# Attention rounds of a hybrid decoder block: the products with V between the two halves of the transposes, the copies of the second half behind the round's end

## The chip, the cores and the metric

The kernel runs on one core of one Trainium2 chip. The metric is the time of one execution in microseconds (us) on the device. Work is spread over five engines that run side by side, each through its own list of instructions in order: TensorE (PE, matmuls and transposes; PEld is its weight load), VectorE (DVE), ScalarE (ACT), GpSimd (POOL) and SyncE (SP, here only the issuer of transfers). They wait for each other through semaphores.

## The reference, cut to what matters

One decoder block on a sequence of 2048 positions and 1024 channels, in float32. One input projection gives the inputs of two branches. Branch A is a causal sliding-window attention in three head groups with dilation 1, 4 and 16, eight heads of 64 channels each; branch B is a convolution with a gated linear recurrence. Both are gated, projected, merged, projected once more and normalised. The change lies in branch A, in this part of the reference:

```python
    s = jnp.einsum('brnqhd,brnkhd->brnhqk', qb, kw) * (Dh ** -0.5)
    ...
    s = jnp.where(valid[None, None, :, None], s, NEG_INF)
    m = jnp.max(s, axis=-1, keepdims=True)
    p = jnp.exp(s - m)
    l = jnp.sum(p, axis=-1, keepdims=True)
    o = jnp.einsum('brnqhk,brnkhd->brnqhd', p, vw)
```

Queries come in blocks of 128 (after the positions are regrouped by the dilation), and each block sees the keys of its own block and of the one before it, 256 in all. Where a block has no block before it (the first of each subsequence, and every block of the group with dilation 16) it sees 128 keys only.

## The kernel before, in words

The kernel has three stages. First the input projection (matmuls in a fast scheme with seven products, L622, with the convolution and the recurrence beside them), then the attention, then the projections of both branches, the merge and the normalisation (from L1305 on). Nothing in the order of instructions is left to a scheduler: every engine runs its instructions in the order in which the program writes them. What can shift is only what they wait for: data, and buffers that come round again.

The attention works through 12 units, one for each dilation group and pair of heads; `unit(u)` takes the groups in the order 1, 16, 4 in turn. Each unit has 2048 queries, cut in four rounds of 512, so there are `NG = 48` rounds; a round has four query blocks j = 0 to 3 and two heads h. The work on one round's data is spread over four rounds of the loop. The names of the steps:

- `scores(i)` (PE, L1005): 24 matmuls into four PSUM tiles "s" (two blocks and one head each). The pool has four such buffers, so the next round's scores wait until the peaks of this round have read them.
- `peak(i, j, h)` (DVE, L1012): adds the mask to one block's scores (kept with reversed sign), writes them to SBUF as "p" and accumulates their minimum. Its operand is 256 or 128 wide, as the block has one before it or not.
- `expo(i, j, h)` (ACT, L1020): the exponential in place on "p", and its sum.
- `turn(i, w)` (PE, L1030): transposes half w of a round (blocks 2w and 2w+1) into two PSUM tiles "pt", k = 0 and 1.
- `bring(i, w, k, eng)` (L1043 on ACT, L1045 on DVE): copies one such tile to SBUF, into "ptb". Of the first half, k = 0 goes to ACT and k = 1 to DVE; of the second half, k = 1 goes to DVE, and k = 0 goes to DVE in the "light" rounds (all of dilation 16, and every third of the others) and to ACT in the others.
- `values(i)` (PE, L1058): the products of "ptb" with V into one PSUM tile "o".
- `leave(i)` (DVE, L1067, L1069, L1071): copies "o" out to SBUF, from where it is sent to memory.

The tiles "pt" and "o" share one pool of PSUM buffers, tag "t", with four buffers that are given out in the order of the program; a round takes five (two, two and one). So a tile takes the buffer of the fourth one before it and waits until that one has been read out.

```python
        t = st["t", i, w] = [aps.tile([P, 2, 2, 2, 64], F32, tag="t", name=f"pt{i}{w}{k}", bufs=4) for k in range(2)]
        o = st["o", i] = aps.tile([P, 4, P], F32, tag="t", name=f"o{i}", bufs=4)
```

In round i of the loop PE has, in this order, the scores of i, the transposes of both halves of i-1, and the products of i-2. ACT has the last three exponentials of i-1, the first of i, the copy of the first half, three exponentials, the copy of the second half (unless the round is light), and one exponential. DVE has the copy-out of i-3, four peaks of i, its copy of the first half, two peaks, in a light round the other copy of the second half, two peaks, and its copy of the second half.

Of the kernel before, what the change touches and what calls it, by code (L numbers as in the profile page):

```python
# [31 lines left out]
def hybrid_block_kernel(ctx: ExitStack, tc: tile.TileContext, a: dict, out: bass.AP):  # L32
    nc = tc.nc
    sp, act, dve, pool, pe = nc.sync, nc.scalar, nc.vector, nc.gpsimd, nc.tensor
# [59 lines left out]
    def later(lag, fn):  # L94
        late.append((now["n"] + lag, fn))
# [4 lines left out]
    def run(queue):  # L100
        due = [x for x in queue if x[0] <= now["n"]]
        queue[:] = [x for x in queue if x[0] > now["n"]]
        for _, fn in due:
            fn()
# [443 lines left out]
    light = [("v", FT_V + 2 * j, FT_V + 2 * j + 1) for j in range(6)]  # L548
# [129 lines left out]
    def at(t, fn):  # L678
        events.setdefault(t, []).append(fn)
# [26 lines left out]
    for s, pl in enumerate(plan):  # L706
        if pl[4] == "ug" and not (pl[0] and pl[1][1][0] - FT_U in put_off):
            at(base[s] + 1, lambda i=pl[1][1][0] - FT_U: fetch_gr(i))
        if pl[0] and pl[4] == "ug":
            i = pl[1][1][0] - FT_U  # L710
# [4 lines left out]
    def keep_raw(b, c, kk):  # L715
        load_raw(b, c, kk, "c")

    def one_block(b, kk):
        if kk == 0:
            new_block(b)  # L720
        hi_lo(b, kk, xr["c" + b, kk])
        spend(ACT=.66, DVE=.72)
# [26 lines left out]
    def bring(t, b, c):  # L749

        at(t - 3, lambda: [keep_raw(b, c, kk) for kk in K4])
        at(t, lambda: [one_block(b, kk) for kk in K4])
# [36 lines left out]
    def unit(u):  # L789

        return (0, 2, 1)[u % 3], u // 3
# [41 lines left out]
    def v_parts(g, j):  # L833
        src = v_scr[g][j]

        def part(i):
            def fn():
                if i == 0:
                    VT[g, j] = big(VSLOT[g, j], [P, 16, 256], F32, f"V{g}{j}")
                V = VT[g, j]  # L840
                if g == 0:
                    sp.dma_start(V[:, 4 * i:4 * i + 4], src[i * CH:(i + 1) * CH].rearrange("(n p) f -> p n f", p=P))
                elif g == 1:
                    sp.dma_start(V[:, 4 * i:4 * i + 4], src[i * CH:(i + 1) * CH].rearrange("(j r) f -> j r f", r=4))
                else:
                    sp.dma_start(V[:, 4 * i:4 * i + 4], src.rearrange("(i r) f -> i r f", r=16)[:, 4 * i:4 * i + 4])
            return fn

        return [part(i) for i in range(4)]
# [115 lines left out]
    def prev(g, n):  # L965
        if g == 0:
            return n - 1 if n >= 1 else None
        if g == 1:
            return n - 4 if n >= 4 else None
        return None  # L970

    st = {}
# [3 lines left out]
    def first(i, j):  # L976
        u, q = divmod(i, 4)
        g, _ = unit(u)
        return 0 if prev(g, 4 * q + j) is not None else P
# [27 lines left out]
    def peak(i, j, h):  # L1007
        u, q = divmod(i, 4)
        lo = first(i, j)
        if h == 0:  # L1010
            st["p", i, j] = p_p.tile([P, 2, 256], F32, tag="p", name=f"p{i}{j}")
        dve.tensor_tensor_reduce(out=st["p", i, j][:, h, lo:256], in0=st["s", i, j // 2][h][:, j % 2, lo:256],  # L1012
                                 in1=mask[:, lo:256], scale=1.0, scalar=3e38, op0=ALU.add, op1=ALU.min,
                                 accum_out=sta[u][:, 4 * q + j, h:h + 1])

    def expo(i, j, h):
        u, q = divmod(i, 4)
        p = st["p", i, j][:, h, first(i, j):256]
        s = sta[u][:, 4 * q + j]
        act.activation(p, p, AF.Exp, scale=-1.0, bias=s[:, h:h + 1], accum_out=s[:, 2 + h:3 + h])  # L1020
# [9 lines left out]
                        pe.transpose(t[k][:, j % 2, x, h, :], pp[j % 2][r, h, x * P:(x + 1) * P], ident[r, r])  # L1030

    def bring(i, w, k, eng):
        if k == 0:
            st["b", i, w] = at_p.tile([P, 2, 2, 2, P], F32, tag="pt", name=f"ptb{i}{w}", bufs=4)
        src = st["t", i, w][k]
        dst = st["b", i, w][..., HALF[k]]
        lo = [first(i, 2 * w + j) // P for j in range(2)]
        if lo[1]:
            dst, src = (t[:, :, 1] for t in (dst, src))
        else:  # L1040
            dst, src = (t.rearrange("p j x h q -> p (j x) h q")[:, lo[0]:] for t in (dst, src))
        if eng is act:
            act.activation(dst, src, AF.Copy)  # L1043
        else:
            dve.tensor_copy(dst, src)  # L1045

    def values(i):
        u, q = divmod(i, 4)
        g, hp = unit(u)
        V = VT[g, hp // 2]  # L1050
        o = st["o", i] = aps.tile([P, 4, P], F32, tag="t", name=f"o{i}", bufs=4)
        for j in range(4):
            ptb = st["b", i, j // 2]
            n = 4 * q + j
            for x in range(first(i, j) // P, 2):
                for h, hs in enumerate(HALF):
                    v0 = P * (hp % 2) + 64 * h
                    pe.matmul(o[hs, j, :], V[:, n if x else prev(g, n), v0:v0 + 64], ptb[:, j % 2, x, h, :],  # L1058
                              start=(x == first(i, j) // P), stop=(x == 1))

    def leave(i):
        u, q = divmod(i, 4)
        g, hp = unit(u)
        o, t = st.pop(("o", i)), ot[u]
        cs = slice(q * CH, (q + 1) * CH)
        if g == 0:
            dve.tensor_copy(t[:, cs].rearrange("p (b q) -> p b q", b=4), o)  # L1067
        elif g == 1:
            dve.tensor_copy(t[:, cs].rearrange("p (j r) -> p j r", r=4), o.rearrange("p r j -> p j r"))  # L1069
        else:  # L1070
            dve.tensor_copy(t.rearrange("p (j r) -> p j r", r=16)[:, :, 4 * q:4 * q + 4], o.rearrange("p r j -> p j r"))  # L1071
        if g < 2:
            later(1, lambda: sp.dma_start(o_scr[g][hp][:, cs], t[:, cs]))
        elif q == 3:
            later(1, lambda: sp.dma_start(o_scr[g][hp], t))
        if q == 3:
            f0 = 4 * (3 * hp + g)
            dst = st_scr[:, f0:f0 + 4]
            if g == 0:
                later(1, lambda: sp.dma_start(dst.rearrange("(n q) f -> q n f", q=P), sta[u]))  # L1080
            elif g == 2:
                later(1, lambda: sp.dma_start(dst.rearrange("(q n) f -> q n f", q=P), sta[u]))
            else:
                for c in range(4):
                    later(1, lambda c=c: sp.dma_start(dst[c * CH:(c + 1) * CH].rearrange("(q r) f -> q r f", r=4),
                                                      sta[u][:, 4 * c:4 * c + 4]))
# [21 lines left out]
    def load_h(c, k, lag):  # L1108
        if k % 4 == 0:
            HH["t"] = big((("X3", "X4"), ("Z0", "Z1"))[c % 2][k // 4], [P, 4, 2, CH], F32R, f"h{c}{k}")  # L1110
        t = HH[c, k] = HH["t"][:, k % 4]
        sp.dma_start(flat(t[:, 1]), hb_scr[k * P:(k + 1) * P, c * CH:(c + 1) * CH])
        later(lag, lambda: split(t[:, 0], t[:, 1], dve if c else pool))

    NG = 48
# [4 lines left out]
    for i in range(NG + 3):  # L1120
        u = i // 4
        on, turns = i < NG, 0 < i <= NG
        run(late)
        if i in VORD:
            loads += v_parts(*VORD[i])
        if i % 4 == 0 and 1 <= u <= 9:
            loads += unit_parts(u + 2)
        for _ in range(2):
            if loads:
                loads.pop(0)()  # L1130
        if on:
            scores(i)
        if i > 2:
            leave(i - 3)
        if turns:
            expo(i - 1, 2, 1)
            expo(i - 1, 3, 0)
            expo(i - 1, 3, 1)
        if on:
            peak(i, 0, 0)  # L1140
            expo(i, 0, 0)
            for j, h in ((0, 1), (1, 0), (1, 1)):
                peak(i, j, h)
        if turns:
            turn(i - 1, 0)
            bring(i - 1, 0, 0, act)
            bring(i - 1, 0, 1, dve)
        if on:
            for j, h in ((0, 1), (1, 0), (1, 1)):
                expo(i, j, h)  # L1150
            peak(i, 2, 0)
            peak(i, 2, 1)
        if turns:
            turn(i - 1, 1)
            light = unit((i - 1) // 4)[0] == 2 or i % 3 == 0
            bring(i - 1, 1, 0, dve if light else act)
        if on:
            peak(i, 3, 0)
            peak(i, 3, 1)
            expo(i, 2, 0)  # L1160
        if turns:
            bring(i - 1, 1, 1, dve)
        if i > 1 and i - 2 < NG:
            values(i - 2)
        if i in (40, 41):
            prep_wl(i - 40, 2)
        if 42 <= i < 46:
            load_h(0, 2 * (i - 42), 2)
            load_h(0, 2 * (i - 42) + 1, 2)
        if i in (46, 47):  # L1170
            prep_wl(i - 44, 2)
        now["n"] += 1
# [308 lines left out]
    for tt in range(16):  # L1481
        c, b = divmod(tt, 4)
# [68 lines left out]
```

## Time and profile before

| | us |
|---|---|
| runs: median (lowest to highest of 3) | 2123.54 (2120.29 to 2123.6) |
| profiled execution, its own time | 2117.73 |
| its span from first to last instruction | 2116.0 |
| PE busy | 2083.6 (98%) |
| DVE busy | 1667.7 (79%) |
| ACT busy | 1123.4 (53%) |
| POOL busy | 490.1 (23%) |

The attention lies between about 1446 and 1659 us of the span: its first scores begin at 1445.7, and the first product of the stage behind it begins at 1658.60. Busy shares over the whole span say little about it, since the three stages have different limits; what is read below is the attention alone. In the answers of the trace a line gives start, duration, engine, line of the program, operation and the tiles written and read; what stands in brackets behind it is the idle time of the engine before it and what ended that. The durations of neighbouring instructions on one engine can overlap: an exponential is shown with 505 ns, while the next one starts 492 ns after it.

### The profile page before, as it was taken

How to read it: one execution, taken by the hardware profiler on the slowest of the kernel's cores; microseconds unless marked ns; L12 is line 12 of the kernel's file. 1: busy time of each engine (PE TensorE's matmuls, PEld its weight loads, DVE VectorE, ACT ScalarE, POOL GpSimd, SP SyncE). 2: the span in 40 equal slices, each digit the busy share in tenths (PEclk: the TensorE clock that was granted, in tenths of full speed). 3: DMA queues.
4: the chain of work that ended last, by engine and by line, in shares of the span. 5: the costliest groups of instructions: out<-in, count | busy, mean ns of one | idle time of the engine just before them, and what ended most of it. 6: DMA issues, size and time to landing. Idle time of an engine off the chain costs nothing.

```text
span 2116.0 us, 35899 instructions
## 1 busy us (share of the span) xinstructions
PE 2083.6 (98%) x12016; PEld 1723.9 (81%) x12016; DVE 1667.7 (79%) x3193; ACT 1123.4 (53%) x2348; POOL 490.1 (23%) x465
## 2 busy tenths in 40 slices
PE   8999999999999999999999999999999999999998
PEld 7888888888878888887888888888888888888887
DVE  8987888898888867787787887777999645576667
ACT  6356455357356565656567766667999411121100
POOL 1111111111111012231231232223535444332120
PEclk9999999999999999999999999999999999999999
DMA  8987997997997977677788788879988788874432
GB/s 271 280 259 225 281 277 212 285 288 230 276 289 230 331 219 202 214 238 211 249 255 269 255 254 265 259 224 383 293 305 260 227 278 282 293 250 158 164 110 70
DMA packets 345832, 524.69 MB, mean 248 GB/s; under 512 B 124208, under 2 KB 153904, under 8 KB 341808
## 3 DMA queue, kind: packets, MB, share of 16 engines
q1 hardware_dynamic: 325760, 489.54, 71.3%
q0 software_dynamic: 12256, 19.42, 5.6%
q10 hardware_dynamic: 7632, 13.44, 1.7%
q8 instruction: 96, 1.57, 0.3%
q14 instruction: 88, 0.72, 0.1%
HBM read 317.14 MB, written 190.45 MB: 240 GB/s over the span
## 4 chain that ended last, share of the span: by engine, by line
PE 64%; ACT 5%; DVE 3%; DMA 1%; issue 1%; SPq 0%; DVEq 0%; ACTq 0%
PE q L622 39%; ACT p L1020 3%; PE yb L1305 3%; PE yb L1306 3%; PE z L1415 3%; PE z L1416 3%; PE yb L1307 3%; PE z L1417 3%; PE ya L1383 1%; PE ya L1384 1%; PE ya L1385 1%; PE o L1058 1%; DVE p L1012 1%; ACT ptb L1043 1%; PE g L492 1%; PE s L1005 1%
## 5 line engine op out<-in xcount | busy, mean ns | idle before, releaser
L622 PE MATMUL q<-xT,hS 128*128 128x512 f32 x1680 | 521.1, 391 | 0.0
L622 PE MATMUL q<-xT,l 128*128 128x512 f32 x1120 | 436.0, 389 | 0.0
L622 PE MATMUL q<-xB,hA 128*128 128x512 f32 x1248 | 389.5, 393 | 5.7 <-ACT xB L215 5.7
L622 PEld LDWEIGHTS q<-xT,hS 128*128 128x128 f32 x1680 | 312.8, 188 | 69.0 <-issue 5.5
L622 PE MATMUL q<-xB,l 128*128 128x512 f32 x904 | 353.0, 391 | 0.0
L622 PEld LDWEIGHTS q<-xB,hA 128*128 128x128 f32 x1248 | 234.0, 189 | 57.2 <-ACT xB L215 5.7
L622 PEld LDWEIGHTS q<-xT,l 128*128 128x128 f32 x1120 | 210.2, 188 | 44.2
L622 PEld LDWEIGHTS q<-xB,l 128*128 128x128 f32 x904 | 170.4, 188 | 36.0
L245 POOL DMA_DIRECT2D wS<-in_w_in_dram x70 | 62.0, 969 | 493.7 <-DMA wS<-in_w_in_dram 139.0
L1020 ACT ACTIVATE p<-p,sta 128x256 f32<-128x256 f32 (+1 forms) x384 | 172.2, 456 | 4.8 <-DVE sta L1012 4.1
L622 PE MATMUL q<-xB,hS 128*128 128x512 f32 x560 | 174.1, 392 | 0.0
L622 PE MATMUL q<-xT,hA 128*128 128x512 f32 x560 | 173.0, 390 | 0.0
L269 ACT ACTIVATE hA<-wA 128x512 fp32r<-128x512 f32 x218 | 134.9, 623 | 53.2 <-DMA wA<-in_w_in_dram 23.8
L269 ACT ACTIVATE hS<-S 128x512 fp32r<-128x512 f32 x175 | 109.0, 623 | 79.4 <-DVE S L227 51.1
L227 POOL TENSOR_TENSOR S<-S,wA 128x512 f32<-128x512 f32 x35 | 45.5, 1299 | 392.8 <-DVE S L227 218.0
L622 PEld LDWEIGHTS q<-xT,hA 128*128 128x128 f32 x560 | 104.7, 188 | 23.0 <-issue 1.5
L622 PEld LDWEIGHTS q<-xB,hS 128*128 128x128 f32 x560 | 104.0, 188 | 22.4 <-issue 1.5
L1012 DVE CUSTOM_DVE_ANT_0 p<-s,mask 128x256 f32<-128x256 f32 (+1 forms) x384 | 118.7, 360 | 4.3 <-PE s L1005 3.3
L1416 PE MATMUL z<-wo,mh 128*128 128x512 f32 (+1 forms) x264 | 101.0, 383 | 0.0
L1417 PE MATMUL z<-wo,ml 128*128 128x512 f32 (+1 forms) x264 | 101.0, 383 | 0.0
L1415 PE MATMUL z<-wo,mh 128*128 128x512 f32 (+1 forms) x264 | 101.0, 383 | 0.0
L1305 PE MATMUL yb<-h,wl 128*128 128x512 f32 x256 | 100.3, 392 | 0.0
(201 smaller groups left out, 4208.5 us busy)
## 6 DMA issues: line engine op xcount, KB each, us to landing
wA<-in_w_in_dram SPq DMA_DIRECT2D x253, 256.0 KB, 4.8
wl_scr<-l SPq DMA_DIRECT2D x105, 512.0 KB, 5.2
l<-wl_scr SPq DMA_DIRECT2D x105, 512.0 KB, 4.7
sw<-y SPq DMA_DIRECT2D x384, 64.0 KB, 3.2
wS<-in_w_in_dram SPq DMA_DIRECT2D x70, 256.0 KB, 4.9
wS<-in_w_in_dram POOLq DMA_DIRECT2D x70, 256.0 KB, 6.2
qh_scr<-hi SPq DMA_DIRECT2D x48, 256.0 KB, 5.7
v_scr<-vs SPq DMA_DIRECT2D x48, 256.0 KB, 4.4
```

What stands on the lines that cost most here:

```text
L227: eng.tensor_tensor(out=out, in0=in0, in1=in1, op=op)
L245: pool.dma_start(t, w_part(s, x), accum_op=ALU.add)
L269: act.activation(h, r, AF.Copy)
L622: pe.matmul(bank, w[:, ks], x[:, kk, xx], start=(first and i == 0), stop=(last and i == 11))
L1012: dve.tensor_tensor_reduce(out=st["p", i, j][:, h, lo:256], in0=st["s", i, j // 2][h][:, j % 2, lo:256], in1=mask[:, lo:256], scale=1.0, s ...
L1020: act.activation(p, p, AF.Exp, scale=-1.0, bias=s[:, h:h + 1], accum_out=s[:, 2 + h:3 + h])
L1305: pe.matmul(yb, WL[f][:, 0, k], xx[:, 0], start=(k == 0), stop=False)
L1306: pe.matmul(yb, WL[f][:, 0, k], xx[:, 1], start=False, stop=False)
L1307: pe.matmul(yb, WL[f][:, 1, k], xx[:, 0], start=False, stop=(k == 7))
L1415: pe.matmul(z, mh[:, k], w[:, 0, hs], start=(k == 0), stop=False)
L1416: pe.matmul(z, mh[:, k], w[:, 1, hs], start=False, stop=False)
L1417: pe.matmul(z, ml[:, k], w[:, 0, hs], start=False, stop=(k == 7))
```

## The change: what it does

Three things move, all in the loop over the rounds; every instruction that was there is still there, on the same engine.

1. `values(i - 2)` now stands between `turn(i - 1, 0)` and `turn(i - 1, 1)` instead of behind both.
2. The copies of the second half of a round are taken out of the round that makes the transposes and put into the next one: on DVE directly behind `leave`, ahead of all peaks; on ACT (where the round isn't light) behind the first of the three exponentials left over.
3. `light` is taken for the round whose copies are made (i - 2 in place of i - 1, and `i % 3 == 1` in place of `i % 3 == 0`), which is the same choice for the same data; the SBUF tile of the copies is made by whichever copy comes first.

```diff
     def bring(i, w, k, eng):
-        if k == 0:
+        if ("b", i, w) not in st:
             st["b", i, w] = at_p.tile([P, 2, 2, 2, P], F32, tag="pt", name=f"ptb{i}{w}", bufs=4)
...
+        copied = 1 < i <= NG + 1
+        light = copied and (unit((i - 2) // 4)[0] == 2 or i % 3 == 1)
         if on:
             scores(i)
         if i > 2:
             leave(i - 3)
+        if copied:
+            bring(i - 2, 1, 1, dve)
+            if light:
+                bring(i - 2, 1, 0, dve)
         if turns:
             expo(i - 1, 2, 1)
+        if copied and not light:
+            bring(i - 2, 1, 0, act)
+        if turns:
             expo(i - 1, 3, 0)
             expo(i - 1, 3, 1)
...
             peak(i, 2, 0)
             peak(i, 2, 1)
+        if i > 1 and i - 2 < NG:
+            values(i - 2)
         if turns:
             turn(i - 1, 1)
-            light = unit((i - 1) // 4)[0] == 2 or i % 3 == 0
-            bring(i - 1, 1, 0, dve if light else act)
         if on:
             peak(i, 3, 0)
             peak(i, 3, 1)
             expo(i, 2, 0)
-        if turns:
-            bring(i - 1, 1, 1, dve)
-        if i > 1 and i - 2 < NG:
-            values(i - 2)
```

How this stands on the engines. First PE in round 4, before: the last transpose of the first half of round 3 ("pt301" is round 3, half 0, k = 1), the second half ("pt310", "pt311"), then the products of round 2 ("o2", from the copied halves "ptb20" and "ptb21").

```order
L1030 MATMUL pt301_14858<-ident_180,p31_14740 128x64
L1030 MATMUL pt310_14884<-ident_180,p32_14767 128x64 [waits DVE_49,Activation_49]
L1030 MATMUL pt311_14885<-ident_180,p32_14767 128x64 [waits DVE_49]
...
L1030 MATMUL pt311_14885<-ident_180,p33_14790 128x64
L1058 MATMUL o2_14909<-ptb20_14761,V00_14369 64x128 [waits Activation_49]
L1058 MATMUL o2_14909<-ptb20_14761,V00_14369 64x128 x5
L1058 MATMUL o2_14909<-ptb21_14788,V00_14369 64x128 x8
```

The same place now:

```order
L1030 MATMUL pt301_14858<-ident_180,p31_14740 128x64
L1058 MATMUL o2_14884<-ptb20_14761,V00_14369 64x128 [waits DVE_49]
L1058 MATMUL o2_14884<-ptb20_14761,V00_14369 64x128 x5
L1058 MATMUL o2_14884<-ptb21_14844,V00_14369 64x128 [waits DVE_49]
L1058 MATMUL o2_14884<-ptb21_14844,V00_14369 64x128 x7
L1030 MATMUL pt310_14901<-ident_180,p32_14767 128x64 [waits Activation_49]
L1030 MATMUL pt311_14902<-ident_180,p32_14767 128x64 [waits Activation_49]
```

The products stood behind a wait for ACT: their buffer was that of "pt300", the fourth tile before them, which ACT copies in the same round. Now their buffer is that of the second half of the round before; what waits for ACT's copy of "pt300" is the second half of the transposes.

Second ACT around the end of round 4, before: exponentials "p40" to "p43" of round 4 and the two copies of round 3 ("ptb30", "ptb31").

```order
L1020 ACTIVATE p40_14850,sta1_14816<-p40_14850,sta1_14816 128x128
L1043 ACTIVATE ptb30_14875<-pt300_14857 128x8x64
L1020 ACTIVATE p40_14850,sta1_14816<-p40_14850,sta1_14816 128x128
L1020 ACTIVATE p41_14854,sta1_14816<-p41_14854,sta1_14816 128x128 x2
L1043 ACTIVATE ptb31_14902<-pt310_14884 128x8x64
L1020 ACTIVATE p42_14881,sta1_14816<-p42_14881,sta1_14816 128x128 x2
L1020 ACTIVATE p43_14904,sta1_14816<-p43_14904,sta1_14816 128x128 x2
```

And now:

```order
L1020 ACTIVATE p40_14850,sta1_14813<-p40_14850,sta1_14813 128x128
L1043 ACTIVATE ptb30_14875<-pt300_14857 128x8x64
L1020 ACTIVATE p40_14850,sta1_14813<-p40_14850,sta1_14813 128x128
L1020 ACTIVATE p41_14854,sta1_14813<-p41_14854,sta1_14813 128x128 x2
L1020 ACTIVATE p42_14881,sta1_14813<-p42_14881,sta1_14813 128x128 x2
L1043 ACTIVATE ptb31_14964<-pt310_14901 128x8x64
L1020 ACTIVATE p43_14919,sta1_14813<-p43_14919,sta1_14813 128x128 x2
```

ACT's copy of the second half moved back by two exponentials. Third DVE at the end of round 3 and the start of round 4, before; round 2 is light, so both copies of its second half ("ptb21") are on DVE. "ot0<-o1" is the copy-out of round 1.

```order
L1012 ISA p32_14767,sta0_14453<-s311_14719,mask_185 128x256
L1045 COPY ptb21_14788<-pt210_14770 128x8x64
L1012 ISA p33_14790,sta0_14453<-s310_14718,mask_185 128x256
L1012 ISA p33_14790,sta0_14453<-s311_14719,mask_185 128x256
L1045 COPY ptb21_14788<-pt211_14771 128x8x64
L1067 COPY ot0_14454<-o1_14795 128x512
L1012 ISA p40_14850,sta1_14816<-s400_14818,mask_185 128x128
```

And now:

```order
L1012 ISA p32_14767,sta0_14453<-s311_14716,mask_185 128x256
L1012 ISA p33_14805,sta0_14453<-s310_14715,mask_185 128x256
L1012 ISA p33_14805,sta0_14453<-s311_14716,mask_185 128x256
L1067 COPY ot0_14454<-o1_14770 128x512
L1045 COPY ptb21_14844<-pt211_14788 128x8x64
L1045 COPY ptb21_14844<-pt210_14787 128x8x64
L1012 ISA p40_14850,sta1_14813<-s400_14815,mask_185 128x128
```

Both copies now stand behind the copy-out, directly ahead of the next round's first peak.

## The prediction

> **What bounds the kernel now.** First the page's 40 slices (52.9 us each), to find the place. The attention fills slices 29 to 31 and parts of 28 and 32.
>
> ```profile
> PE   8999999999999999999999999999999999999998
> DVE  8987888898888867787787887777999645576667
> ACT  6356455357356565656567766667999411121100
> ```
>
> PE is full everywhere else; in the attention DVE and ACT are full as well. So this stage is read by itself. The starts of the scores in PE's timeline repeat every 12 rounds (three units): 1516.08 and 1567.98 open the same round of two neighbouring periods, 51.90 us apart, and 48 rounds are four periods. Next the busy time of each engine in three periods (columns: PE, PEld, DVE, ACT, POOL, granted clock, DMA share, GB/s):
>
> ```profile
> 1464.18:1516.08 51.90, 47.99 (x890) 43.96 (x888) 50.07 (x238) 50.58 (x211) 29.61 (x32) 1.00 0.95 332
> 1516.08:1567.98 51.90, 48.21 (x890) 44.12 (x888) 50.07 (x238) 50.70 (x211) 16.38 (x18) 1.00 0.89 297
> 1567.98:1619.89 51.91, 48.15 (x892) 44.11 (x890) 50.08 (x238) 50.70 (x211) 24.85 (x28) 1.00 0.90 303
> ```
>
> All three engines are near their limit, ACT nearest. Then who waits for whom between 1464 and 1620 us (total, times, longest):
>
> ```profile
> PEld o L1058 <- ACT ptb L1043: 15.7, 36, 0.7
> PE o L1058 <- ACT ptb L1043: 10.3, 33, 0.6
> ACT p L1020 <- DVE sta L1012: 2.9, 7, 0.6
> DVE ot L1067 <- PE o L1058: 2.9, 6, 0.5
> ```
>
> PE stands before the products in every round, 0.44 us on average (15.7 / 36; the second row is the same wait seen by the matmuls). That is the wait the change is about, but PE is the engine with most room, so what counts is whether ACT and DVE pay for it. They do, where blocks get narrow. Two such rounds:
>
> ```profile
> 1520.73 1.56 PE L1005 MATMUL s<-B,A 64*128 64x128 f32 x24
> 1522.13 0.68 PE L1030 MATMUL pt<-ident,p 64*128 64x64 f32 x16
> 1523.03 1.97 PE L1058 MATMUL o<-ptb,V 128*64 128x128 f32 x32 [0.22 <-ACT ptb L1043]
> 1524.93 1.56 PE L1005 MATMUL s<-B,A 64*128 64x128 f32 x24
> 1525.96 0.29 DVE L1012 CUSTOM_DVE_ANT_0 p<-s,mask 128x128 f32<-128x128 f32 x1 [0.22 <-PE s L1005]
> 1526.17 0.28 DVE L1012 CUSTOM_DVE_ANT_0 p<-s,mask 128x128 f32<-128x128 f32 x1
> 1526.29 0.40 ACT L1020 ACTIVATE p<-p,sta 128x128 f32<-128x128 f32 x1 [0.62 <-DVE sta L1012]
> 1526.32 0.68 PE L1030 MATMUL pt<-ident,p 64*128 64x64 f32 x16
> 1526.79 0.38 ACT L1043 ACTIVATE ptb<-pt 128x256 f32<-128x256 f32 x1
> 1527.07 0.39 ACT L1020 ACTIVATE p<-p,sta 128x128 f32<-128x128 f32 x1
> 1527.22 1.09 PE L1058 MATMUL o<-ptb,V 128*64 128x128 f32 x16 [0.22 <-ACT ptb L1043]
> ```
>
> Here the round is a closed loop: from the scores (1524.93) 1.03 us to the first peak, 0.33 to the first exponential, 0.50 to the copy, 0.43 to the products (1527.22), and from there to the next scores the time of the products. With the 1.90 us of the wide products in the round before (1523.03 to 1524.93) that is 1.03 + 0.33 + 0.50 + 0.43 + 1.90 = 4.19, and the round from 1520.73 to 1524.93 took 4.20. ACT's own work in it is less, and so it stands idle at 1526.29.
>
> **What the change is worth, by ACT's work.** It removes and adds no instruction; the light rounds stay the same for the same data. So the gain can only be idle time of the engine that is full, and I count that engine's work in a period. The by-form groups in 1516.08 to 1567.98 give the counts (the window's edge takes one exponential of the next period, so 54 wide, 42 narrow), and the chain of waits gives start to start when nothing waits (ten pieces are five exponentials with the reading of their sums):
>
> ```profile
> L1020 ACT ACTIVATE p<-p,sta 128x256 f32<-128x256 f32 x55 | 27.3, 505 | 0.3 <-DVE sta L1012 0.3
> L1020 ACT ACTIVATE p<-p,sta 128x128 f32<-128x128 f32 x42 | 16.3, 394 | 0.8 <-DVE sta L1012 0.6
> L1043 ACT ACTIVATE ptb<-pt 128x512 f32<-128x512 f32 x11 | 6.4, 584 | 0.1
> L1043 ACT ACTIVATE ptb<-pt 128x256 f32<-128x256 f32 x5 | 1.9, 371 | 0.0
> 1511.19 2.46 ACT p L1020 x10
> 1510.71 0.48 ACT ptb L1043
> 1527.17 3.07 ACT p L1020 x16
> ```
>
> A wide exponential costs 2.46 / 5 = 0.492, a narrow one 3.07 / 8 = 0.384, a wide copy 0.48, a narrow one 0.28 (1526.79 to 1527.07), and one copy of 384 between them, say 0.37. ACT: 54 x 0.492 + 42 x 0.384 + 11 x 0.48 + 0.37 + 5 x 0.28 = 26.6 + 16.1 + 5.3 + 0.4 + 1.4 = 49.8. The period is 51.9: ACT loses 2.1 us of it, more than its idle column shows, because durations overlap the wait behind them.
>
> [...]
>
> **The same for the other engines,** since the gain can't exceed theirs:
>
> ```profile
> L1012 DVE CUSTOM_DVE_ANT_0 p<-s,mask 128x256 f32<-128x256 f32 x55 | 20.3, 419 | 0.1
> L1012 DVE CUSTOM_DVE_ANT_0 p<-s,mask 128x128 f32<-128x128 f32 x42 | 10.0, 286 | 0.7 <-PE s L1005 0.4 <-ACT p L1020 0.3
> 1500.15 0.34 DVE p L1012
> 1500.50 0.60 DVE ptb L1045
> 1534.32 0.34 DVE ptb L1045
> 1574.93 1.97 PE o L1058 x32
> 1576.90 1.49 PE s L1005 x24
> 1569.54 0.56 PE pt L1030 x16
> ```
>
> DVE: 54 wide peaks at 0.34, 42 narrow at 0.21 (1525.96 to 1526.17), 31 copies (16 of 0.60 at most, 15 narrow of 0.34) and 12 copy-outs at 0.60 like the wide copies: 18.4 + 8.8 + 9.6 + 5.1 + 7.2 = 49.1, idle 2.8. PE: 300 products at 1.97 / 32, 288 scores at 1.49 / 24, 300 transposes at 0.56 / 16: 18.5 + 17.9 + 10.5 = 46.9. ACT has the least room, DVE 0.7 us more.
>
> **Which of ACT's 2.1 us go.** The loop above loses its products: they no longer wait for the copy of the same round, the second half of the transposes does, with 1.90 us of products between. Of the 4.20 us round, PE's own work stays: 1.40 to the transposes, 8 x 0.035 = 0.28 for their first half, 1.90, 0.28: 3.86. The scores come 0.34 earlier, and ACT's first exponential with them. Some small gaps of ACT I leave: from 1526.29 to the copy at 1526.79 it took 0.50 where 0.384 is the rule, and three or four of these make, as an estimate, 0.35 a period. So 1.8 of 2.1 go, over four periods 7.2 us.
>
> **New waits, checked in wide rounds.** The pieces: from the first half's last transpose to its copy 0.19 (1526.32 to 1526.79, less 0.28); wide transposes of one half 0.56; scores to first peak 1.1 (1.03 when narrow; an estimate); peak to exponential 0.33 and the 0.13 that a wide peak lasts longer (419 against 286 ns), 0.46. (a) The second half of the transposes waits for ACT's copy of the first half, and the next scores stand behind it. From that copy's end to the next round's first exponential PE's way is 0.56 + 1.1 + 0.46 = 2.1, and DVE's way, with the moved copies, 0.56 + 0.19 + 0.60 (+ 0.60 when light) + 0.46, at most 2.4. Meanwhile ACT has seven exponentials, 7 x 0.492 = 3.4. Spare: 1.0 us. (b) ACT's copy of the second half comes five exponentials (2.46) after that of the first and needs 0.56 + 0.19 of transposes: spare 1.7. (c) Copy, products, transposes, copy as a ring: 0.6 + 1.90 + 0.56 + 0.19 = 3.3, in rounds of 4.5 and more of ACT's work. None closes, so I take 0 for all three; bounds are a gain of ACT's whole 2.1 on one side and on the other the price of (a) in the last rival. (d) At the end, the copies of round 47's second half used to lie under 1.9 us of products; now nothing is between, and one copy of about 0.6 (584 ns in its row) is bare: -0.65 once with its signal. No transfer is added, and the copy-outs stay first on DVE, so the stores on SP's queue shift with their round.
>
> Sum: 7.2 - 0.65 = 6.5 us. The profiled execution took 2117.7 (span 2116.0), so 2111.2 for one like it; its runs' median is 2123.5, which gives **2117.0 us**.
>
> Behind the stage the gain must not be lost:
>
> ```profile
> 1650.79 1.29 POOL L1097 TENSOR_TENSOR h<-h 128x512 fp32r<-128x512 f32 x1
> 1658.60 0.50 PE L1305 MATMUL yb<-h,wl 128*128 128x512 f32 x1
> 1672.93 0.69 DVE L1311 SCALAR_TENSOR_TENSOR gB<-gB,yb 128x512 f32<-128x512 f32 x1 [13.52 <-DMA gB<-mg_scr]
> ```
>
> POOL ends the last operand of the first product at 1652.1. PE would come at 1652.1 and use that operand last, so this holds even if POOL didn't move; its work is issued with the rounds and moves as well. The first result waits for a load behind the last stores, which move with the round.
>
> **Rivals.**
>
> [...] 0.07.
>
> *ACT can't be packed tighter than its busy time.* By the busy view ACT is idle only 51.9 - 50.7 = 1.2 a period. Less 0.35: 0.85 x 4 - 0.65 = 2.8, 2120.7 us, no change to be told. Against: the 2.46 us chain shows starts closer than ends. 0.15.
>
> *The gain is given back behind the stage*, by the loads that stand behind the last stores (13.52 us of DVE waiting, of which PE has seen nothing so far, having four result buffers): 2123 us. 0.05.
>
> *Slower: DVE's copies starve ACT.* They now stand ahead of all peaks. [...] A copy whose transposes are late (they now follow the products) holds up every peak, the scores' buffers and the first exponential. It decides once (a)'s spare 1.0 us is gone, when DVE's way exceeds 3.4 us; if it were then 0.5 over in each of 28 wide rounds, 14 us are lost: 2123.5 - 6.5 + 14 = 2131 us. Against: DVE's way adds up to 2.4, and ACT has work queued. 0.08.
>
> **How the numbers follow.** Forecast 0.65. Faster by over 0.2% (4.2 us, about what a measurement of this kernel tells from no change): 0.65 + 0.07 = 0.72; same: 0.15 + 0.05 = 0.20; slower 0.08. Unknown inside the forecast: a quarter more or less of 2.1 us a period (2 us) and the runs' spread of 3 us. The range is 2113.5 to 2121.5: the DVE rival, the forecast and the busy-time rival lie in it.
>
> **What would show it.** The period of the scores 50.1 to 50.3 us in place of 51.9; the wait of the products for ACT's copies gone, a smaller one of the transposes (L1030) in its place; ACT's idle before exponentials near 0; the round after the first narrow one near 3.9 us; the stage's end 6 to 7 us earlier and the rest as long as before. Wrong would be: ACT waiting for DVE's peaks in wide rounds (then DVE's copies were too early), a period unchanged with PE waiting less (then PE's wait cost nothing), or an end that doesn't follow the stage's.

## The result

| | median (lowest to highest), us | runs |
|---|---|---|
| before | 2118.94 (2115.79 to 2123.60) | 14 |
| after | 2114.45 (2111.59 to 2117.71) | 14 |

The ratio is 0.9976, with a 95% interval of 0.9967 to 0.9984: faster by 5.1 us (3.4 to 7.0). The forecast was 6.5 us less and 2117.0. The time lies 2.6 us under it: the kernel before, over 14 runs, has a median 4.6 us lower than the three that the forecast began from, and 2.0 us less were gained than forecast by the medians (4.5 of 6.5).

The profiled execution has a span of 2112.0 us, 4.0 less than before. Only 2.1 of these are the attention's: from its first scores to the first product of the next stage it takes 210.8 us (1443.77 to 1654.60) where it took 212.95. The other 1.9 us lie ahead of it, in a stage that the change doesn't touch; in the thirteen profiles of this document the first scores come anywhere between 1443.5 and 1445.9 us, whatever the edit. What lies behind is as long as before, 457.4 us in both. So the profile asks two questions: why the stage gained 2.1 us and not 6.5, and why the median over many executions shows more than this one.

### The profile page after: what moved, and what is told of

It reads as the page before. It is cut to its first block, busy times and chain, and to the rows that moved or that the text cites. A ratio compares the mean times of both kernels' runs of the same rounds, so it can differ in the third digit from the quotient of the medians.

```text
span 2112.0 us, 35853 instructions
## 1 busy us (share of the span) xinstructions
PE 2088.6 (99%) x12016; PEld 1729.0 (82%) x12016; DVE 1663.8 (79%) x3193; ACT 1120.5 (53%) x2348; POOL 491.9 (23%) x465
## 4 chain that ended last, share of the span: by engine, by line
PE 91%; ACT 6%; DVE 2%; DMA 1%; issue 0%; SPq 0%
PE q L622 66%; ACT p L1020 5%; PE yb L1310 3%; PE yb L1311 3%; PE z L1420 3%; PE z L1421 3%; PE z L1422 3%; PE yb L1312 3%; PE ya L1388 1%; PE ya L1389 1%; PE ya L1390 1%; PE g L492 1%; PE vtp L358 1%; ACT ptb L1043 1%; PE o L1058 1%; DVE p L1012 1%
```

## The profile after

The timeline of PE gives both ends of the stage: round 0 opens it, round 47 starts at 1642.14, and the first product of the next stage ends it (its line number is 5 higher now).

```profile
1443.77 0.32 PE L1005 MATMUL s<-B,A 64*128 64x128 f32 x1
1642.14 0.36 PE L1005 MATMUL s<-B,A 64*128 64x256 f32 x1
1653.58 1.09 PE L1058 MATMUL o<-ptb,V 128*64 128x128 f32 x16 [0.41 <-DVE ptb L1045]
1654.60 0.50 PE L1310 MATMUL yb<-h,wl 128*128 128x512 f32 x1
```

The busy time of each engine in the three periods from round 4 to round 40 (columns: window and its length, PE, PEld, DVE, ACT, POOL, granted clock, DMA share, GB/s):

```profile
1460.86:1510.64 49.78, 48.89 (x895) 44.87 (x892) 48.85 (x234) 49.78 (x210) 25.32 (x28) 1.00 0.94 331
1510.64:1560.43 49.79, 48.88 (x896) 44.86 (x892) 49.13 (x236) 49.79 (x210) 19.19 (x21) 1.00 0.89 289
1560.43:1616.06 55.63, 52.09 (x897) 47.66 (x892) 49.25 (x234) 50.39 (x210) 26.03 (x29) 0.94 0.93 314
```

Two periods fell from 51.90 to 49.8, less than forecast (50.1 to 50.3), and ACT is busy in every microsecond of them: the whole 2.1 us that it lost are gone, not 1.8. The third is 5.8 us longer. Who waits for whom between 1460 and 1612 us (total, times, longest) shows where:

```profile
DVE ot L1071 <- issue: 4.1, 1, 4.1
PEld pt L1030 <- DVE ot L1071: 3.6, 1, 3.6
PEld pt L1030 <- ACT ptb L1043: 2.8, 13, 0.5
PEld o L1058 <- ACT ptb L1043: 1.5, 4, 0.4
ACT p L1020 <- DVE sta L1012: 4.3, 2, 3.7
```

The products' wait for ACT's copies, 15.7 us over 36 rounds before, is down to 1.5, and 2.8 of the transposes stand in its place. The first row is new: one copy-out waits 4.1 us, PE behind it 3.6, and ACT's 4.3 lie behind the same place (1571 to 1590 us). It is that of round 28, first in DVE's list in round 31. DVE, PE and SP there:

```profile
1571.78 0.29 DVE L1012 CUSTOM_DVE_ANT_0 p<-s,mask 128x128 f32<-128x128 f32 x1
1576.20 0.69 DVE L1071 COPY ot<-o 128x512 f32<-128x512 f32 x1 [4.12 <-issue]
1576.95 0.46 PE L1030 MATMUL pt<-ident,p 64*128 64x64 f32 x7 [3.43 <-DVE ot L1071]
1541.49 12.21 SPq L846 DMA_DIRECT2D V<-v_scr  x1
1564.13 0.32 SPq L1073 DMA_DIRECT2D o_scr<-ot  x1
```

The program has two SBUF buffers "ot" for the copy-outs, one for each unit (four rounds) in turn. Unit 7 begins in round 28, and so its first copy-out needs the buffer of unit 5, whose last store SP issued at 1564.13. The copy-out started 12.1 us later, and could have started at 1572.1, when the peaks ahead of it were done. Before, the same two rows were 14.3 us apart, and nothing waited:

```profile
1566.24 0.32 SPq L1073 DMA_DIRECT2D o_scr<-ot  x1
1580.57 0.68 DVE L1071 COPY ot<-o 128x512 f32<-128x512 f32 x1
```

The store came 2.1 us sooner, the copy-out wanted its buffer 8.5 us sooner (1580.57 to 1572.1); of both, 1.9 is the earlier start of the stage. Round 31 and the next take 7.51 and 5.35 us in place of the 3.15 and 3.35 of the same rounds a period earlier, and the rounds behind them win back 0.5.

The trace also has the landing of that one store (issue to landing, three times the same number, as it is one store), first in this kernel, then before:

```profile
DMA to landing us min/median/max: 12.0/12.0/12.0
```

```profile
DMA to landing us min/median/max: 11.7/11.7/11.7
```

Before, 14.3 - 11.7 = 2.6 us were spare. The copy-out came 8.5 - 2.1 = 6.4 us nearer to its store and the landing took 0.3 longer: 6.4 - 2.6 + 0.3 = 4.1 us, the wait.

The wait isn't all that the stall costs. In round 32 no copy-out waits for its buffer, and yet it is 2.0 us longer. The same narrow round a period earlier and round 32 (columns as above; PE's granted clock is the third number from the end), and 24 narrow scores in round 31, ahead of the wait, and in round 32:

```profile
1525.24:1528.59 3.35, 3.30 (x63) 2.92 (x60) 3.35 (x23) 3.35 (x20) 3.19 (x5) 1.00 0.97 388
1579.41:1584.76 5.35, 5.35 (x62) 4.90 (x60) 3.78 (x23) 4.41 (x22) 1.81 (x2) 0.52 1.04 413
1571.90 1.54 PE L1005 MATMUL s<-B,A 64*128 64x128 f32 x24
1579.41 2.80 PE L1005 MATMUL s<-B,A 64*128 64x128 f32 x24
```

PE's granted clock is 0.52 in round 32, its scores take 2.80 us in place of 1.54, and PE is busy in all of the round. This and the 0.89 of round 31 (1571.90 to 1579.41) are where the 0.94 of the third period comes from.

## Experiments

The numbers of all runs, each beside runs of the kernel before on the same chip; the period is that of the scores over twelve rounds without a stall, the stage goes from first scores to first product behind it. Where only one time was taken, the ratio is left out.

| kernel | period | stage | ratio (95%) |
|---|---|---|---|
| before | 51.90 | 212.95 | |
| after | 49.8, one 55.6 | 210.8 | 0.9976 (0.9967 to 0.9984) |
| after, again | 49.8, one stalled | 212.4 | 0.9984 (0.9976 to 0.9993) |
| products moved alone | 52.50 | 216.4 | 1.0003 (0.9994 to 1.0012) |
| copies moved alone | 54.21 | 224.2 | 1.0042 (1.0028 to 1.0055) |
| before, three output buffers | 51.9 | 213.0 | 0.9998 (0.9989 to 1.0008) |
| after, three output buffers | 49.8 to 50.3 | 205.8 | 0.9963 (0.9951 to 0.9976) |
| the same, five buffers of sums | 49.8 | 205.0 | 0.9961 (0.9948 to 0.9975) |
| after, one kind of statistics store off SP | 49.8, one 52.0 | 207.2 | 0.9961 (0.9948 to 0.9975) |
| after, all statistics stores off SP | 49.8 | 205.0 | 0.9953 (0.9939 to 0.9967) |
| three buffers, fewer light rounds | 51.0 | 208.9 | |
| three buffers, every round light | 52.0 | 213.2 | |
| three buffers, a quarter of the exponentials short | 49.4 | not read | |

### The two parts alone

The products between the halves, with the copies of the second half left at the round's end:

```diff
+        if i > 1 and i - 2 < NG:
+            values(i - 2)
         if turns:
             turn(i - 1, 1)
...
-        if i > 1 and i - 2 < NG:
-            values(i - 2)
```

> The kernel before with the first part of the change alone: the products between the two halves of the transposes, all copies where they were. Theory Q (each engine's list in order): the copy of the second half at the end of DVE's round now waits for transposes that stand behind 1.9 us of products, the next round's peaks and the scores' buffers stand behind it, and ACT behind the peaks. Walking the three lists with the rows' durations gives a period of 54.0 us (51.9 before) and about 8 us more in all: 2127. Rival W: the wait of the products for ACT's copy was the price, and taking it away gives most of the gain by itself: period 50 to 51, 4 us less than before.

The period is 52.50, between the two numbers: 1.5 us under the higher and 1.5 over the lower, so the sign was right with the first theory and the size with neither. Time: no change (1.0003). The chain of waits over that period by line, and the waits in it:

```profile
by line: PE o L1058 32.7%; PE s L1005 29.7%; PE pt L1030 21.4%; DVE p L1012 6.7%; DVE ptb L1045 5.3%; issue 3.0%; DVE sta L1012 0.6%; DVE ot L1071 0.5%; DVEq L1071 0.1%
PEld s L1005 <- DVE sta L1012: 3.3, 11, 0.8
DVE ptb L1045 <- PE pt L1030: 2.5, 4, 1.0
```

PE now carries the chain, and in no round does it wait for ACT's copies before the products. But DVE's copy, last in its round, waits for transposes that now stand behind the products (1.97 us for 32 of them), and the next scores wait for the peaks behind it.

The copies behind the round's end, with the products left where they were:

```diff
-        if i > 1 and i - 2 < NG:
-            values(i - 2)
         if turns:
             turn(i - 1, 1)
...
             expo(i, 2, 0)
+        if i > 1 and i - 2 < NG:
+            values(i - 2)
```

> The changed kernel with the products back behind both halves of the transposes; only the copies of the second half stay moved into the next round. Theory Q: the buffers of the transposes come free a round later, the copy-out of the products (first on DVE) waits for products that still end PE's round, and now two or three copies stand between it and the first peak; walking the lists gives a period of 54.5 us and about 11 us more than before: 2130. Rival W: the copies only change places with peaks and exponentials of the same length, so nothing changes: period 51.9.

The period is 54.21, near the 54.5 expected, and the time 0.4% longer. The waits in one period:

```profile
PEld o L1058 <- ACT ptb L1043: 7.5, 12, 0.9
ACT p L1020 <- DVE sta L1012: 3.4, 5, 1.0
```

The products wait for ACT's copy in each of the 12 rounds, 7.5 us where it was 5.1 before. So neither part gains anything: alone they cost 0.6 and 2.3 us a period, together they save 2.1.

### The stall in round 31

First the changed kernel once more, unchanged:

> The changed kernel itself once more, for the copy-out's wait for its store. Theory S: it belongs to the change. A round of some 7 us stands again in one of the periods near 1575 us, the stage is again 4 to 6 us longer than with three buffers. Rival C: it comes in some executions only; then this profile may show 49.8 us in all periods, and the stage some 205 us.

The stall is there again, in the same round, with 4.34 us, and in the round behind it 24 narrow scores take 2.80 us (1580.68), where ahead of the wait they took 1.53 (1572.44). The stage takes 212.4 us: the rounds of the stall cost 1.2 us more than in the first profile, and a later round 0.9. So the stall stands in both profiled executions of this kernel. Over eleven runs it is faster by 0.16%, which is the edge of the first comparison's interval.

Three output buffers in place of two:

```diff
-            ot[u] = at_p.tile([P, S], F32, tag="ot", name=f"ot{u}")
+            ot[u] = at_p.tile([P, S], F32, tag="ot", name=f"ot{u}", bufs=3)
```

> The changed kernel with three buffers in place of two for the tile into which the products are copied out (8 KB more of SBUF in each partition). In the profile of the change one copy-out waited 4.12 us at 1572 us, and the rounds from 1571.90 to 1616.06 took 5.8 us more than the same rounds of the period before; all other rounds repeat every 49.8 us. Theory S (store): the wait is for the store out of that buffer two units earlier, and it belongs to the change, not to that one execution. Then with a third buffer the wait is gone, all periods are 49.8, the stage from the first scores to the first product behind it takes about 205 us (210.8 in the change, 212.95 before), and the time is 4 to 6 us below the change, about 9 us below before (ratio 0.9957). Rival C (chance): the wait happens in few executions. Then the time is that of the change, ratio 0.9976.

No copy-out waits for a buffer any more, the stage takes 205.8 us, 7.1 less than before, and the time falls by 0.37%. What is left are two longer rounds, one of them behind a wait of 0.7 us for a buffer of the sums. The same edit on the kernel before:

> The kernel before with three buffers for the copy-out tile. Theory S: before, the copy-out came 14.3 us after the issue of that store and never waited, so nothing changes: period 51.9, time within 0.2% of before. Rival: the third buffer gains by itself (transfers spread otherwise), and then what it gains in the changed kernel isn't the wait.

Nothing: 0.9998, and the period stays 51.9. The third buffer is worth something only to the rounds of the changed kernel. Five buffers of the sums as well (`bufs=5` for "sta" in place of 3):

> Three buffers for the copy-out tile, and five in place of three for the small tile of extremes and sums (sta), whose store a first peak waited for (0.7 us, twice) with three copy-out buffers. Theory S: what is left of waits for stores goes, the stage is 205.0 to 205.3 us (205.8 with three and three), the time 0.5 us lower than there, about 2111 on runs where before is 2119.5. Rival: that wait is not what lengthened the rounds at 1523 and 1593 us (loads of the next unit are), and nothing changes.

All three full periods are 49.8 and the stage 204.97 us, the lower end of what was expected; the time (0.9961) can't be told from that with three output buffers.

That takes the wait away, but doesn't tell why SP was late. In the changed kernel and in the one before, the issue right behind a store of a dilation-16 unit's statistics (2048 rows of 16 bytes) takes 8.8 to 12.4 us in three of four places: the row of 12.21 above stands 1.2 us behind that store. So the store itself was moved to GpSimd's queue:

```diff
             elif g == 2:
-                later(1, lambda: sp.dma_start(dst.rearrange("(q n) f -> q n f", q=P), sta[u]))
+                later(1, lambda: pool.dma_start(dst.rearrange("(q n) f -> q n f", q=P), sta[u]))
```

> The changed kernel with two output buffers as it is, only that the store of the statistics of the units of dilation 16 (L1082) is issued by GpSimd's queue in place of SP's; nothing is left out of the computation. Theory P: on SP's queue the issue right behind that store takes 12.2 to 12.9 us in the kernel before and in the changed one alike (1542 and 1593 us), this is what makes the following stores of `ot` late, and so what makes the copy-out of round 31 wait 4.1 us; with the store off SP's queue no issue of 12 us stands there, the copy-out does not wait, and the stage takes 205 to 207 us, as with three buffers, 7 to 9 us under the kernel before, a ratio of 0.9957 to 0.9967. Rival: SP is late for another reason (its own order, or transfers that land late whatever stands ahead of them); then the long issue or the wait stays, the stage takes 210 to 212.5 us, and the ratio is 0.9975 to 0.9985. If GpSimd's queue is held up by the store in SP's place, what GpSimd issues behind it comes 12 us late, and it would show as a wait for its loads or memsets.

The wait of round 31 is gone with two buffers; the ratio is as the first theory has it, the stage 0.2 us above its range. Another copy-out waited instead, in round 35, for 1.7 us; behind it 32 products took 3.46 us (1590.37) in place of 1.97, and the period is 2.2 us longer:

```profile
1560.33 7.72 SPq L1085 DMA_DIRECT2D st_scr<-sta  x4
1578.62 8.45 SPq L816 DMA_DIRECT2D B<-k_scr  x2
1588.98 0.69 DVE L1069 COPY ot<-o 128x512 f32<-128x512 f32 x1 [1.69 <-DMA o_scr<-ot]
```

SP still spends 7.7 us on the four statistics stores of a dilation-4 unit, and 8.45 on two loads behind the one of a dilation-1 unit. So all of them went to GpSimd's queue (the same edit at L1080 and L1085):

> The changed kernel with two output buffers as it is, and the stores of the statistics of all units (L1080, L1082, L1085) issued by GpSimd's queue in place of SP's; nothing is left out. With those of dilation 16 alone moved, one wait of 1.7 us for an output buffer was left in round 35; ahead of the store that it waited for, SP spent 7.7 us on the four statistics stores of dilation 4 (1560 us), and behind those of dilation 1 8.5 us on two loads (1579 us). Theory P: these too make SP late; with all of them gone no copy-out waits for an output buffer, no stretch of SP's queue between 1460 and 1640 us has issues of 6 us, and the stage takes 205.0 to 206.0 us, ACT's work and nothing else (1.2 to 2.2 us under the run with one kind moved, 7 to 8 us under the kernel before; ratio 0.9955 to 0.9967). Rival: SP is late from its loads' own waiting for buffers; the wait of round 35 and the 8 us on two loads stay, the stage takes 207 us or more. A second rival: GpSimd's queue, which works through its list in order and waits up to 24 us for its loads, sends the statistics late; then DVE's peaks wait for a buffer of the sums (L1012 behind the statistics store) for some us in all, and the stage takes 207 to 210.

No copy-out waits for its buffer, the stage is 204.97 us and the ratio 0.9953 (2108.45 us): 10 us under the kernel before (8.0 of them are the stage's in the profile) and the lowest ratio of all that ran, though the intervals overlap. The last store of unit 5, issued at 1564.13 in the changed kernel, goes out 6.3 us sooner here, more than the 4.1 us that the copy-out had waited:

```profile
1557.85 0.32 SPq L1073 DMA_DIRECT2D o_scr<-ot  x1
```

SP's issues of L1073 between 1440 and 1640 us (count: shortest/median/longest in ns), first in the changed kernel, then in this one:

```profile
L1073 SPq DMA_DIRECT2D o_scr<-ot x28: 319/416/12307, 1464.1 to 1626.6; - x28
```

```profile
L1073 SPq DMA_DIRECT2D o_scr<-ot x29: 319/319/665, 1463.2 to 1638.2; - x29
```

Without the statistics' stores on its queue, no store of "ot" takes SP longer than 0.67 us. And the chain of waits over one period of this last kernel:

```profile
by line: ACT p L1020 84.8%; ACT ptb L1043 14.1%; issue 1.9%; ACTq L1020 0.1%
```

Before, in the period from 1516.08, the same line was a mixture:

```profile
by line: ACT p L1020 38.2%; PE o L1058 13.7%; ACT ptb L1043 11.5%; DVE p L1012 11.4%; PE s L1005 10.3%; DVE ptb L1045 5.4%; issue 4.2%; PE pt L1030 2.3%; DVE ot L1071 1.8%; DVE sta L1012 0.8%; DVE ot L1069 0.7%; DVEq L1012 0.0%
```

Now no other engine stands in it.

### What bounds the stage now

The measured 2114.4 us are also what a bound by DVE would give from DVE's idle time before: 2.8 us a period, less 0.35 for small gaps, 4 x 2.45 - 0.65 = 9.1 us off the 2123.5 that the forecast began from. So the mechanism has to be told apart from the number. All three runs are the kernel with three output buffers. First ACT gets more copies and DVE fewer (in dilation 1 and 4 no round is light):

```diff
-        light = copied and (unit((i - 2) // 4)[0] == 2 or i % 3 == 1)
+        light = copied and unit((i - 2) // 4)[0] == 2
```

> Three copy-out buffers, and in the groups with dilation 1 and 4 all copies of the second half's first tile on ACT: 2.33 copies a period go from DVE to ACT. Theory A (ACT's work sets the period, 49.8 us): 49.8 + 2.33 x 0.48 = 50.9, a little more by new waits, 51.2. Rival D (DVE's work sets it): the period falls below 49.8, since DVE loses 1.4 us of work.

Then the reverse (`light = copied`, every copy of a second half on DVE):

> Three copy-out buffers, and all copies of the second half on DVE: 4.67 copies a period go from ACT to DVE. DVE's work is then 49.1 + 4.67 x 0.60 = 51.9, ACT's 47.6. Theory A with DVE close behind: the period follows DVE, 51.9 to 52.6, no better than before the change. Rival (ACT alone is the bound, DVE has room in time that counts): the period falls to 47.6 to 49.

One period of each, columns as above:

```profile
1518.87:1569.87 51.00, 48.69 (x895) 44.55 (x892) 48.65 (x233) 51.00 (x215) 19.87 (x22) 1.00 0.93 313
```

```profile
1564.89:1616.90 52.01, 51.43 (x895) 45.84 (x892) 52.01 (x241) 48.13 (x205) 24.23 (x27) 1.00 0.90 302
```

With more copies ACT is busy for all of 51.00 us, and the period is ACT's work; with fewer, DVE is busy for all of 52.01, and the period is DVE's. The share that the change was built on lies between: ACT full, DVE 49.13 of 49.79.

Last, ACT's exponentials of every fourth block cut short, which takes about 2 us of its work away and nothing of DVE's:

```diff
+        if j == 3:
+            p = p[:, 0:64]
```

> The changed kernel with three output buffers, whose exponentials of the fourth block of a unit run over 64 columns in place of their full width, with a weaker mask value (30), so that nothing overflows: part of the exponentials is left out, and the attention's values are others than the reference's. It takes some 2.05 us of 49.9 off ACT's work in a period of twelve rounds, and nothing off DVE's 49.1 or PE's 46.9. Theory C (after the change ACT and DVE bound the stage together, within 1 us of each other): the period falls by 0 to 0.8 us only, to 49.1 to 49.8. Rival D (ACT alone sets the pace, and DVE's waits give way): the period falls by what ACT loses, to 47.7 to 48.2.

```profile
1509.60:1558.98 49.38, 48.95 (x896) 44.84 (x892) 49.13 (x236) 47.43 (x210) 20.25 (x22) 1.00 0.86 277
ACT p L1022 <- DVE sta L1012: 1.9, 3, 0.8
```

The period falls by 0.4 us only, to 49.38: at 49.13 of busy time DVE is all but full, and ACT waits for its peaks. (The third period of this run has waits of 4.1 us for buffers of the sums and isn't read.) So a bound by DVE has the order of the two the wrong way round by a hair: ACT sets the period, and DVE stands 0.4 to 0.7 us behind it.

## Why the prediction was right, and where it was not

**The bound (ACT's work).** Right. Its work was put at 49.8 us a period, and the undisturbed periods are 49.78 and 49.79; the chain of the last kernel is ACT from end to end. DVE's 49.1 was right as well: 49.13 in the period shown and in the run with short exponentials, where DVE is all but full. PE's 46.9 was put to no test.

**"So 1.8 of 2.1 go".** A little too small: all of the 2.1 go, since the small gaps of ACT that I left, an estimate of 0.35 us a period, closed too. Over four periods that is 8.4 instead of 7.2; less the end's loss it gives 7.8, and the stage is 8.0 us shorter where nothing stalls (212.95 to 204.97). The single round that I worked out, 3.86 us in place of 4.20, came out at 3.96 (1515.11 to 1519.07): the half of the transposes ahead of the products takes 0.42 to the products' start, not the 0.28 of eight times 0.035.

**The new waits (a), (b), (c).** Right at 0: the transposes' wait for ACT's copy is there, 0.2 us on average (2.8 over 13 times) and 0.5 at most, and ACT doesn't wait behind it. That the products alone, or the copies alone, gain nothing was not said in the forecast; the spare times were checked for both together only.

**The end (d).** Right: -0.65 forecast; from the last round's scores to the next stage it takes 0.68 us longer (12.46 for 11.78), with the bare wait of 0.41 us in the row at 1653.58.

**"No transfer is added, and the copy-outs stay first on DVE, so the stores on SP's queue shift with their round."** This step failed. The stores shift with their round only while SP isn't late, and SP was late: the issue at 1541.49, right behind a store of statistics, took 12 us in both kernels, whatever the rounds did, and in both the last store of unit 5 came 22 to 23 us behind that issue. The copy-out's demand moved 8.5 us forward where the store moved 2.1, and the slack of the two buffers was gone: 4.1 us of waiting, and with the round at a granted clock of 0.52 behind it 5.8 us of the period. The trace of before had it all, issues of 12 us behind statistics stores (L1082; the one shown is three units later) and, in its list of transfers, the median from a store's issue to its landing:

```profile
1596.35 0.67 SPq L1082 DMA_DIRECT2D st_scr<-sta  x1
1597.11 12.41 SPq L1073 DMA_DIRECT2D o_scr<-ot  x1
```

```profile
o_scr<-ot SPq DMA_DIRECT2D x32, 256.0 KB, 9.2
```

From the store's issue to the next use of its buffer it was 14.3 us there. The median landing, 9.2 us, leaves 5.1 of them spare, but this store took 11.7 and the longest of the 32 in that trace 15.3. So only 2.6 us were spare, and the copy-out came 6.4 us nearer to its store.

So the forecast's 6.5 is the right mechanism with two errors of opposite sign: 1.5 us too little from the rounds (8.0 without a stall), and a stall not foreseen. That the two partly cancel, and that the measured time lies within the range though the kernel before was 4.6 us faster than the runs that the forecast began from, is luck. In both profiled executions the stall takes 5.8 us or more, which leaves 2.1 and 0.5 us of gain; the medians show 5.1 (3.4 to 7.0) and 3.4 (1.5 to 5.1). Why the medians show more than the profiled executions isn't settled: that the stall is shorter or absent in some executions would do it, but no run shows the stall of an execution that wasn't profiled.

**The rivals.** No run of the changed kernel shows DVE as the bound, which 0.07 of the chances and the 2113.5 to 2121.5 of the range take in: ACT was busy for 49.79 of 49.79 us, DVE for 49.13. That ACT can't be packed tighter than its busy time fell with ACT busy for 49.79 of 49.79 us. The loss behind the stage did not come (457.4 us in both). That DVE's copies starve ACT is what happens when the copies are moved alone, where ACT waits 3.4 us a period for DVE's sums and the period grows, as it was said, but not in the change as a whole. The peak at 1525.96 in the kernel before is a weak sign of such a hold-up: it came after the copy-out (1525.05, 0.69 us), but what it waited for last, 0.22 us, was PE's scores.

## What to carry to other kernels

When three engines lie within a few per cent of each other, count each one's work in a period from start-to-start times; where a wait off the fullest engine is taken away, the gain is that engine's idle time and no more, and it may need two moves together that lose when made alone. Before forecasting that a faster loop stays fast, list every buffer that is handed to a transfer inside it, and compare the time from its issue to its next use with the longest time from issue to landing in the trace (here 14.3 with 15.3 us), not with the median. A stall can cost more than its wait: here 4.1 us of waiting were followed by a round with a granted clock of 0.52, 2.0 us longer. A queue that only issues transfers can be the late one: look for issues that take far longer than their neighbours (here up to 12.3 us for a store of "ot", where the median is 0.42), and at what was issued right before them.

## What the runs showed of the hardware

**Behind a store of 2048 rows of 16 bytes SP's next issue took up to 12.3 us.** The store takes SP 0.4 to 1.6 us itself, but the next issue on SP, of a load or of a store, took 11.2 us (L1073), 12.2 (L846) and 12.3 (L1073) behind three of the four stores of dilation-16 units in the changed kernel, and 4.8 (L1105) behind the fourth; behind those of dilation-1 units it took up to 8.3 (L816). As these have as many rows of the same size, the size of the rows alone doesn't set the time. On GpSimd's queue one such store costs 1.1 us, and the four of a dilation-4 unit, one right behind the other, 2.9 in all, where SP took 7.7 (1560.33 above):

```profile
1588.48 1.12 POOL L1082 DMA_DIRECT2D st_scr<-sta  x1
1605.53 2.94 POOL L1085 DMA_DIRECT2D st_scr<-sta  x4
```

The packets differ as well. The queues' part of the page, in the changed kernel and in the one with all statistics stores on GpSimd:

```profile
q1 hardware_dynamic: 325760, 489.54, 71.5%
q0 software_dynamic: 12256, 19.42, 5.5%
```

```profile
q1 hardware_dynamic: 300800, 489.14, 71.4%
q0 software_dynamic: 13152, 19.81, 5.8%
```

With twelve units' statistics moved from SP to GpSimd, q1 loses 24,960 packets, about 2,080 for each unit's 2,048 rows, and q0 gains 896: about 75 for a unit. The issue behind such a store took up to 12.3 us on SP's queue, more than the 9.1 us in which a store of "ot" lands in the median of the changed kernel. Why the issue behind is held up was not tried further.

**PE's granted clock fell behind the stall.** In the kernel before it was 1.00 from 1470 to 1640 us, and in seven variants 1.00 in the periods read; no wait of a matmul there was longer than 0.74 us. After PE had waited 3.4 us in round 31 of the changed kernel it was 0.52 for the 5.35 us of round 32. In three other runs PE's work took longer behind a wait: in the second profile of the changed kernel, after 3.7 us, 24 narrow scores took 2.80 us in place of 1.53; with one kind of statistics store moved, after 1.4 us, 32 products took 3.46 in place of 1.97; and with the short exponentials, after 2.5 us, 16 products took 1.47 in place of 1.09 (1582.22) and the granted clock of that period was 0.97. That the idle PE is the reason is argued from this order; no run changed PE's idle time alone.

**ACT's durations are longer than its pitch, and they grew as its period filled.** The wide exponentials' mean duration in a period was 505 ns before and is 631 after, the narrow ones' 394 and 489, with the same work and the same pitch (0.492 us from start to start in wide rounds), while ACT's busy time went from 50.70 of 51.90 us to 49.79 of 49.79. After, the by-form groups of 1510.64 to 1560.43:

```profile
L1020 ACT ACTIVATE p<-p,sta 128x256 f32<-128x256 f32 x55 | 28.9, 631 | 0.0
L1020 ACT ACTIVATE p<-p,sta 128x128 f32<-128x128 f32 x42 | 17.2, 489 | 0.0
```

Had the forecast used the durations of before, it would have found ACT's work longer than the period: 54 x 0.505 + 42 x 0.394 + 11 x 0.584 + 5 x 0.371 = 52.1 us of 51.90, without the copy of 384 columns.
